# Attention probabilities of every second unit transposed by VectorE in 32x32 blocks and moved by SBUF transfers

## The chip, the cores and the metric

The kernel runs on one NeuronCore of one Trainium2 chip. The metric is the device time of one execution in microseconds (us), the median of several runs. Engines are named as the profile names them: PE is TensorE's matmuls and PEld its weight loads, DVE is VectorE, ACT is ScalarE, POOL is GpSimd, SP is SyncE, which only issues transfers.

## The reference

One encoder layer is computed for two inputs, a prompt of 1024 tokens and a sample of 512, in float32 with D_MODEL = 1024. `_token_mixer` has two branches. Branch A is grouped-query attention: 8 query heads of 64, two key/value heads, no mask. The change is in branch A.

```python
def _gqa_attention(q, k, v):
    ...
    def block(qi):
        s = jnp.einsum('bqkgd,bskd->bkgqs', qi, k, preferred_element_type=jnp.float32) * scale
        p = jax.nn.softmax(s, axis=-1)
        return jnp.einsum('bkgqs,bskd->bqkgd', p.astype(v.dtype), v)
...
    merged = jax.nn.sigmoid(ga) * (o_a @ w_proj_a) + jax.nn.sigmoid(gb) * (o_b @ w_proj_b)
    return merged @ w_out
...
    h = h + _token_mixer(_rmsnorm(h, norm_mix_g[l]), ...)
    h = h + jnp.square(jax.nn.relu(hn @ w_mlp_up[l])) @ w_mlp_down[l]
    return _rmsnorm(h, norm_final_g)
```

Branch B is attention over a neighbourhood of the token grid; a feed-forward part follows for both inputs together.

## The kernel before

Matmuls work on pairs of numbers: a value is split into a high part (a copy rounded to the type fp32r, made by ACT) and a low part (the value less the high part, a subtraction on DVE). A product takes two or three matmuls with such parts (`mm3`, lines 194 to 197, takes three).

The work runs as two trunks, first the sample (512 tokens, tile names with `s0`), then the prompt (1024 tokens, `s1`), and then the feed-forward part (`mlp`). A trunk runs branch A for its two groups of four heads (g = 0, 1), then branch B, then the merge. Each group of branch A has a stage phR, which projects and rotates queries, keys and values and writes `qT` (two tiles, one for even and one for odd heads), `kT` and `vhl`, and a stage phA, the attention, which is the stage of the change. So there are four phA stages: two for the sample, two for the prompt.

In phA a unit is one head and 512 queries: 4 units for the sample, 8 for the prompt, in the order of `units`. `NT` is the number of 128-key chunks, 4 or 8; `NB` is the number of 512-token blocks, 1 or 2.

- `s_tile(u, j)` makes the probabilities for 128 queries: score matmuls into a PSUM tile of the pool "big" (two buffers), the row maximum on DVE (line 743), the exponential on ACT (line 746, which reads PSUM and frees it), the reciprocal of the sum on DVE (line 748) and the scaling in place on POOL (line 749). The result is a P tile, 128 queries x all keys, from 8 buffers.
- For each chunk `kc` of keys, four transposes on TensorE (line 783) bring keys onto partitions, in a PSUM tile of the pool "mm" (four buffers). ACT copies the high part `hi` (`pth`, line 788, three buffers), DVE subtracts the low part `lo` (`ptl`, line 789, three buffers).
- `pv` multiplies chunk `kc` with the values, two matmuls into the unit's output (lines 759 and 760). It runs LAG = 2 chunks behind. After the last chunk `finish_o` adds both halves and stores the output.
- While a unit's chunks are worked off, `s_tile` for the next unit is put in at chunks 0, 1, 3 and 4 (prompt) or 0, 0, 1 and 2 (sample).
- `fill` gives TensorE other work between: the columns of the gate projection, generator `gate` (line 408). One `pull` is one `mm3`, three matmuls with 512 columns. A gate column has weights of its own (`w_g`, loaded on SP by `load_cols`, line 223, and cut into high and low part at lines 184 and 190) and ends each 512-token block with line 429. A phA stage works on four columns.

Large tiles come from `slot(...)`: the pool `s8r` on the right-hand side has `NRIGHT` = 11 buffers of 8 KB per partition; `slot_left` takes from another pool with 6. From the right-hand pool come `qT`, `kT`, `vhl`, the weights of the gate columns, the weights of the next stage (`wgh` and `wgl` of the second group, four tiles; `w_bq`, `w_bk` and the value strips `vs` for branch B), and for the prompt two of the eight tiles with its normalised input (`xhl`).

The order of instructions on each engine isn't the order of the program text: the framework orders the program when it is built, by priority and by its own estimate of when operands and buffers are there, and it gives a buffer to an instruction that is ready when the buffer is free, also to one that stands later in the text. Each engine then runs its list strictly in that order, and SP issues its transfers strictly in order too.

Of the kernel before, what the change touches and what calls it, by code (L numbers as in the profile page):

```python
# [15 lines left out]
ALU = mybir.AluOpType  # L16
# [45 lines left out]
def encoder(ctx: ExitStack, tc: tile.TileContext, xs, outs, w):  # L62
# [24 lines left out]
    def slot(shape, dt, name, left=False):  # L87
        return (s8l if left else s8r).tile(shape, dt, tag="s8", name=name)
# [4 lines left out]
    def mm(name):  # L93
        return pmm.tile([P, 512], F32, tag="mm", name=name)
# [301 lines left out]
    def run(tr, nxt, first):  # L396
# [100 lines left out]
        for g in range(2):  # L497
# [229 lines left out]
                setup_bias()  # L727
            with phase(f"phA{N}_{g}") as ph:
                units = [(h, qb) for h in range(4) for qb in range(NB)]
                PP = {}  # L730

                def s_tile(u, j):
                    h, qb = u
                    nm = f"{N}_{g}_{h}_{qb}_{j}"
                    q0 = (qb * 4 + j) * P
                    lhs = qT[h % 2][:, h // 2, q0 : q0 + P]
                    s = big(f"s{nm}")[:, :T]
                    for kb in range(NB):
                        ks = slice(kb * 512, kb * 512 + 512)
                        nc.tensor.matmul(s[:, ks], lhs, kT[:, 0, ks], start=True, stop=False)  # L740
                        nc.tensor.matmul(s[:, ks], lhs, kT[:, 1, ks], start=False, stop=True)  # L741
                    nm_ = sml.tile([P, 1], F32, tag="nm", name=f"nm{nm}")
                    nc.vector.tensor_reduce(nm_, s, axis=AX.X, op=ALU.max, negate=True)  # L743
                    p = ph.tile([P, T], F32, tag="P", name=f"p{nm}", bufs=8)
                    l = sml.tile([P, 1], F32, tag="l", name=f"l{nm}")
                    nc.scalar.activation(p, s, AF.Exp, bias=nm_, accum_out=l)  # L746
                    rl = sml.tile([P, 1], F32, tag="rl", name=f"rl{nm}")
                    nc.vector.reciprocal(rl, l)  # L748
                    nc.gpsimd.tensor_scalar(p, p, rl, 1.0, op0=ALU.mult, op1=ALU.mult)  # L749
                    PP[u, j] = p  # L750

                o_of = {}

                def pv(u, kc, hi, lo):
                    h, qb = u
                    if kc == 0:
                        o_of[u] = mm(f"o{N}_{g}_{h}_{qb}")
                    o = o_of[u]
                    nc.tensor.matmul(o, vhl[:, kc, :], hi, start=(kc == 0), stop=False)
                    nc.tensor.matmul(o, vhl[:, kc, :], lo, start=False, stop=(kc == NT - 1))  # L760
                    if kc == NT - 1:
                        r0 = (g * 4 + h) * HD
                        finish_o(o, 512, oad[r0 : r0 + HD, qb * 512 : qb * 512 + 512], ph, f"A{N}_{g}_{h}_{qb}")

                for j in range(4):
                    s_tile(units[0], j)
                    fill.pull(2)
                queue = []
                LAG = 2
                for ui, u in enumerate(units):  # L770
                    h, qb = u
                    if first:
                        bias_row(g * 4 + ui)
                        if g == 0 and ui == 1:
                            early["a"] = load_a(1)
                        if g == 0 and ui == 2:
                            early["v"] = load_v(1, slot)
                    nxt_u = units[ui + 1] if ui + 1 < len(units) else None
                    sdone = 0
                    for kc in range(NT):  # L780
                        pt = mm(f"pT{N}_{g}_{h}_{qb}_{kc}")
                        for j in range(4):
                            nc.tensor.transpose(  # L783
                                pt[:, j * P : (j + 1) * P], PP[u, j][:, kc * P : (kc + 1) * P], ident
                            )
                        hi = ph.tile([P, 512], F32R, tag="pth", name=f"pth{N}_{g}_{h}_{qb}_{kc}", bufs=3)
                        lo = ph.tile([P, 512], F32R, tag="ptl", name=f"ptl{N}_{g}_{h}_{qb}_{kc}", bufs=3)
                        nc.scalar.activation(hi, pt, AF.Copy)  # L788
                        nc.vector.tensor_tensor(lo, pt, hi.bitcast(F32), op=ALU.subtract)  # L789
                        queue.append((u, kc, hi, lo))  # L790
                        if nxt_u is not None:
                            while sdone < 4 and kc >= ((0, 1, 3, 4) if NB == 2 else (0, 0, 1, 2))[sdone]:
                                s_tile(nxt_u, sdone)
                                sdone += 1

                        fill.pull(1 if NB == 1 or kc % 4 < 3 else 0)
                        if len(queue) > LAG:
                            pv(*queue.pop(0))
                fill.drain()
                for item in queue:  # L800
                    pv(*item)
# [994 lines left out]
```

## Time and profile before

| | |
|---|---|
| median of 3 runs | 2145.62 us (2144.97 to 2146.48) |
| span of the profiled execution, first to last instruction | 2144.2 us |
| around that span, against the median of the runs | 1.4 us |
| mean granted TensorE clock | 0.999 |
| busy: PE, PEld, DVE, ACT, POOL | 99%, 86%, 68%, 53%, 17% |
| transposes of line 783 | 640, in 160 groups of four |
| high parts, line 788, and low parts, line 789 | 160 each |
| tiles of probabilities (line 749) | 64 of 128x1024, 32 of 128x512 |

The rows of the views are read like this. In a group's row stand the line, the engine and operation, what it writes and reads, partitions x elements and type, the count, then busy us and the mean ns of one, then the engine's idle time just before these instructions and what ended it. In a timeline's row stand the start in us from the span's start, the length, and the same names; x4 means that four instructions in a row are shown as one piece. In a row of stretches the busy us of PE, PEld, DVE, ACT and POOL follow each other with the number of instructions in brackets, then the granted clock (1.00 is full), the share of time the transfer engines were busy, and GB/s. Matmuls are pipelined, so their busy times overlap, and what a matmul costs is read from the distance of starts.

### The profile page before, as it was taken

To read this page: it belongs to the slowest core of one execution; us is meant where nothing else is said; L and a number is where in the kernel's file an instruction comes from. 1 tells how busy PE (TensorE), PEld (TensorE's weight loads), DVE (VectorE), ACT (ScalarE), POOL (GpSimd) and SP (SyncE) were. 2 spreads that over 40 slices of the span, in tenths; PEclk is the share of its full clock that TensorE was granted. 3 is DMA by queue.
4 is the path that set the end of the run, shared out by engine and by line. 5 is a ranking of instruction groups with operands and counts; after the bars stand their busy time and mean duration, and the time that the engine had idled before them with its cause. 6 is when DMAs were issued, how large, how long until landed. Compare 5 with 4: busy or idle time off the path is not lost.

```text
span 2144.2 us, 32083 instructions
## 1 busy us (share of the span) xinstructions
PE 2116.2 (99%) x10967; PEld 1847.3 (86%) x10967; DVE 1462.7 (68%) x2793; ACT 1146.2 (53%) x2511; POOL 356.1 (17%) x446
## 2 busy tenths in 40 slices
PE   9999999999999999999999999999999999999998
PEld 8888778888897888887888899999999988888886
DVE  6665786767657755656882877777777777659563
ACT  6664653767566644555530566566655643434342
POOL 2232310323232223333200200003000000000000
PEclk9999999999999999999999999999999999999999
DMA  6437557520122133444472665578545799688561
GB/s 190 133 98 212 152 162 251 186 71 25 57 79 68 42 95 108 131 118 112 140 240 103 213 194 184 171 248 205 165 142 157 256 353 343 212 279 281 165 206 59
DMA packets 321259, 354.08 MB, mean 165 GB/s; under 512 B 31551, under 2 KB 255431, under 8 KB 321095
## 3 DMA queue, kind: packets, MB, share of 16 engines
q1 hardware_dynamic: 277927, 279.65, 41.9%
q10 hardware_dynamic: 36016, 52.19, 7.0%
q0 software_dynamic: 7152, 20.19, 3.5%
q8 instruction: 87, 1.43, 0.3%
q14 instruction: 77, 0.63, 0.1%
HBM read 264.85 MB, written 87.88 MB: 165 GB/s over the span
## 4 chain that ended last, share of the span: by engine, by line
PE 67%; DVE 1%; issue 1%; DMA 0%; ACT 0%; POOL 0%; SPq 0%; POOLq 0%; ACTq 0%; DVEq 0%
PE dn L195 6%; PE dn L196 6%; PE dn L197 6%; PE ua L195 2%; PE ua L196 2%; PE ua L197 2%; PE ud L195 2%; PE ud L196 2%; PE ud L197 2%; PE uc L195 2%; PE uc L196 2%; PE uc L197 2%; PE gpss L195 2%; PE gpss L197 2%; PE gpss L196 2%; PE ops L197 1%
## 5 line engine op out<-in xcount | busy, mean ns | idle before, releaser
L197 PE MATMUL dn<-wd,al 128*128 128x512 f32 x624 | 242.8, 389 | 0.0
L196 PE MATMUL dn<-wd,ah 128*128 128x512 f32 x624 | 242.8, 389 | 0.0
L195 PE MATMUL dn<-wd,ah 128*128 128x512 f32 x624 | 242.7, 389 | 0.0
L1273 ACT ACTIVATE ah<-ar 128x512 fp32r<-128x512 f32 x168 | 104.4, 628 | 203.1 <-PE dn L196 177.1
L1274 DVE TENSOR_TENSOR al<-ar,ah 128x512 fp32r<-128x512 f32 x168 | 113.9, 685 | 71.6 <-ACT ah L1273 64.0
L197 PEld LDWEIGHTS dn<-wd,al 128*128 128x128 f32 x624 | 117.1, 188 | 24.4
L195 PEld LDWEIGHTS dn<-wd,ah 128*128 128x128 f32 x624 | 117.1, 188 | 24.3
L196 PEld LDWEIGHTS dn<-wd,ah 128*128 128x128 f32 x624 | 117.1, 188 | 24.2
L749 POOL TENSOR_SCALAR ps<-ps,rls 128x1024 f32<-128x1024 f32 (+1 forms) x96 | 96.8, 1010 | 225.7 <-DVE rls L748 200.4
L788 ACT ACTIVATE pths<-pTs 128x512 fp32r<-128x512 f32 x160 | 94.0, 597 | 74.0 <-PE pTs L783 71.9
L789 DVE TENSOR_TENSOR ptls<-pTs,pths 128x512 fp32r<-128x512 f32 x160 | 107.6, 686 | 37.7 <-ACT pths L788 36.9
L743 DVE TENSOR_REDUCE nms<-ss 128x1 f32<-128x1024 f32 (+1 forms) x96 | 99.8, 1040 | 25.6 <-PE ss L741 25.0
L195 PE MATMUL gpss<-xs_0h,w_gs 128*128 128x512 f32 x256 | 105.5, 412 | 0.5 <-DVE ot_Bs L440 0.4
L746 ACT ACTIVATE ps<-ss,nms 128x1024 f32<-128x1024 f32 (+1 forms) x96 | 93.2, 972 | 22.8 <-DVE nms L743 20.2
L783 PEld LDWEIGHTS pTs<-ident,ps 128*128 128x128 f32 x640 | 77.9, 140 | 28.5 <-POOL ps L749 4.3
L180 POOL TENSOR_TENSOR rs_f<-ms_f,mhalf 128x1 f32<-128x1 f32 x6 | 4.0, 667 | 590.7 <-DVE ms_f L176 590.7
L197 PE MATMUL gpss<-xs_0h,w_gs 128*128 128x512 f32 x256 | 101.1, 395 | 0.2 <-DVE w_gs L190 0.2
L196 PE MATMUL gpss<-xs_0l,w_gs 128*128 128x512 f32 x256 | 101.0, 394 | 0.0
L783 PE MATMUL pTs<-ident,ps 128*128 128x128 f32 x640 | 99.0, 274 | 1.3 <-DVE ptls L789 0.6
L1273 ACT ACTIVATE A<-S 128x512 fp32r<-128x512 f32 x128 | 75.9, 623 | 31.5 <-DVE S L1336 22.7
L957 POOL TENSOR_TENSOR bms<-rects,msks 128x384 f32<-128x384 f32 (+1 forms) x72 | 70.1, 977 | 129.1 <-DVE nmbs L974 107.6
L1392 ACT ACTIVATE c<-c 128x384 f32<-128x384 f32 x96 | 50.3, 524 | 69.4 <-DVE c L1391 69.3
(330 smaller groups left out, 6419.7 us busy)
## 6 DMA issues: line engine op xcount, KB each, us to landing
ar<-ud SPq DMA_DIRECT2D x120, 512.0 KB, 5.3
br<-in_w_mlp_down_dram SPq DMA_DIRECT2D x72, 512.0 KB, 5.2
rawu<-in_w_mlp_up_dram SPq DMA_DIRECT2D x64, 512.0 KB, 4.1
ud<-c ACTq DMA_DIRECT2D x128, 192.0 KB, 3.2
raw_gs<-in_w_in_dram SPq DMA_DIRECT2D x32, 512.0 KB, 4.0
zgs<-sgs ACTq DMA_DIRECT2D x48, 256.0 KB, 2.2
ud<-cs SPq DMA_DIRECT2D x64, 192.0 KB
raw_os<-in_w_out_dram SPq DMA_DIRECT2D x16, 512.0 KB, 3.9
```

What stands on the lines that cost most here:

```text
L195: nc.tensor.matmul(out, ah, bh, start=start, stop=False, **kw)
L196: nc.tensor.matmul(out, ah, bl, start=False, stop=False, **kw)
L197: nc.tensor.matmul(out, al, bh, start=False, stop=stop, **kw)
L743: nc.vector.tensor_reduce(nm_, s, axis=AX.X, op=ALU.max, negate=True)
L746: nc.scalar.activation(p, s, AF.Exp, bias=nm_, accum_out=l)
L749: nc.gpsimd.tensor_scalar(p, p, rl, 1.0, op0=ALU.mult, op1=ALU.mult)
L783: nc.tensor.transpose(pt[:, j * P : (j + 1) * P], PP[u, j][:, kc * P : (kc + 1) * P], ident)
L788: nc.scalar.activation(hi, pt, AF.Copy)
L789: nc.vector.tensor_tensor(lo, pt, hi.bitcast(F32), op=ALU.subtract)
L957: nc.gpsimd.tensor_tensor(bm.rearrange("p (r c) -> p r c", c=32), rects[h][:, ir : ir + kr_n, jr : jr + 32], msk[:, hf * 3 + ct, :].rearra ...
L1273: nc.scalar.activation(hi, src, AF.Copy)
L1274: nc.vector.tensor_tensor(lo, src, hi.bitcast(F32), op=ALU.subtract)
```

## The change

Every second unit in the order of `units` (`moved`: numbers 1, 3, 5, 7) gets its chunks of keys without TensorE and PSUM.

- The unit's four tiles of probabilities go into one tile `PM` (16 KB per partition for the prompt, one buffer), in an order in which 32-key blocks stand by their place b within a chunk, then by chunk, then by query tile j. The exponential writes in that order, the scaling on POOL is done in place as before.
- `blocks_t`: DVE transposes every 32x32 block of tile j in place (`nc.vector.transpose`).
- `spread_t`: when the fourth tile is done, transfers on SP's queue carry each of the 16 combinations of 32-partition blocks (b, a) to its partitions in a tile `PX`, 64 KB each, 2 KB per partition. There is one PX tile for four chunks, so 16 transfers for a sample unit and 32 for a prompt unit. PX tiles come from `slot`, the right-hand pool with 11 buffers.
- `chunk_hl`: for a moved unit ACT copies the high part from PX, and POOL, not DVE, subtracts the low part from PX.
- P tiles of the other units have 4 buffers, not 8.
- The order of `s_tile` becomes `ahead`: 1, 0, 3, 2, 5, 4, 7, 6. Two units are made before the first chunk (with one `pull` after each tile, eight in all as before); then a unit's probabilities are made during the chunks of the unit two earlier in that order: 3 during 0, 2 during 1, and so on.

```diff
-                PP = {}
+                PP, PX = {}, {}
+                moved = {u: i % 2 == 1 for i, u in enumerate(units)}
...
-                    p = ph.tile([P, T], F32, tag="P", name=f"p{nm}", bufs=8)
                     l = sml.tile([P, 1], F32, tag="l", name=f"l{nm}")
-                    nc.scalar.activation(p, s, AF.Exp, bias=nm_, accum_out=l)
                     rl = sml.tile([P, 1], F32, tag="rl", name=f"rl{nm}")
+                    if moved[u]:
+                        if j == 0:
+                            PP[u] = ph.tile([P, 4, NT, 4, 32], F32, tag="PM", name=f"pm{nm}", bufs=1)
+                        p = PP[u][:, :, :, j, :]
+                        nc.scalar.activation(
+                            p.rearrange("p b k i -> p k b i"),
+                            s.rearrange("p (k b i) -> p k b i", b=4, i=32),
+                            AF.Exp,
+                            bias=nm_,
+                            accum_out=l,
+                        )
+                        p = p.rearrange("p b k i -> p (b k) i")
+                    else:
+                        p = PP[u, j] = ph.tile([P, T], F32, tag="P", name=f"p{nm}", bufs=4)
+                        nc.scalar.activation(p, s, AF.Exp, bias=nm_, accum_out=l)
                     nc.vector.reciprocal(rl, l)
                     nc.gpsimd.tensor_scalar(p, p, rl, 1.0, op0=ALU.mult, op1=ALU.mult)
-                    PP[u, j] = p
+
+                def blocks_t(u, j):
+                    p = PP[u][:, :, :, j, :].rearrange("p b k i -> p (b k) i")
+                    nc.vector.transpose(p, p)
+
+                def spread_t(u):
+                    h, qb = u
+                    PX[u] = []
+                    for q in range(NT // 4):
+                        t = slot([P, 4, 4, P], F32R, f"px{N}_{g}_{h}_{qb}_{q}")
+                        PX[u].append(t.bitcast(F32))
+                        for b in range(4):
+                            for a in range(4):
+                                nc.sync.dma_start(
+                                    PX[u][q][b * 32 : b * 32 + 32, a].rearrange("p k q -> p (k q)"),
+                                    PP[u][a * 32 : a * 32 + 32, b, q * 4 : q * 4 + 4].rearrange("p k j i -> p (k j i)"),
+                                )
+
+                def chunk_hl(u, kc, hi, lo):
+                    h, qb = u
+                    if moved[u]:
+                        src = PX[u][kc // 4][:, :, kc % 4, :].rearrange("p a (j i) -> p a j i", j=4)
+                        hv, lv = (t.rearrange("p (j a i) -> p a j i", j=4, a=4) for t in (hi, lo))
+                        nc.scalar.activation(hv, src, AF.Copy)
+                        nc.gpsimd.tensor_tensor(lv, src, hv.bitcast(F32), op=ALU.subtract)
+                        return
+                    pt = mm(f"pT{N}_{g}_{h}_{qb}_{kc}")
+                    for j in range(4):
+                        nc.tensor.transpose(pt[:, j * P : (j + 1) * P], PP[u, j][:, kc * P : (kc + 1) * P], ident)
+                    nc.scalar.activation(hi, pt, AF.Copy)
+                    nc.vector.tensor_tensor(lo, pt, hi.bitcast(F32), op=ALU.subtract)
...
-                for j in range(4):
-                    s_tile(units[0], j)
-                    fill.pull(2)
+                ahead = [u for i in range(0, len(units), 2) for u in (units[i + 1], units[i])]
+
+                def s_step(u, j):
+                    s_tile(u, j)
+                    if moved[u]:
+                        blocks_t(u, j)
+                        if j == 3:
+                            spread_t(u)
+
+                for i in range(2):
+                    u = ahead.pop(0)
+                    for j in range(4):
+                        s_step(u, j)
+                        fill.pull(1)
...
-                    nxt_u = units[ui + 1] if ui + 1 < len(units) else None
+                    nxt_u = ahead.pop(0) if ahead else None
...
-                        pt = mm(f"pT{N}_{g}_{h}_{qb}_{kc}")
-                        for j in range(4):
-                            nc.tensor.transpose(
-                                pt[:, j * P : (j + 1) * P], PP[u, j][:, kc * P : (kc + 1) * P], ident
-                            )
                         hi = ph.tile([P, 512], F32R, tag="pth", name=f"pth{N}_{g}_{h}_{qb}_{kc}", bufs=3)
                         lo = ph.tile([P, 512], F32R, tag="ptl", name=f"ptl{N}_{g}_{h}_{qb}_{kc}", bufs=3)
-                        nc.scalar.activation(hi, pt, AF.Copy)
-                        nc.vector.tensor_tensor(lo, pt, hi.bitcast(F32), op=ALU.subtract)
+                        chunk_hl(u, kc, hi, lo)
...
-                                s_tile(nxt_u, sdone)
+                                s_step(nxt_u, sdone)
```

## The prediction

> **What bounds the kernel now.** I read the page first, then the busy time by stage, the instructions grouped by form in the stage of the change, TensorE's timeline, and last who held the tile buffers. The page: TensorE is busy throughout, at full clock.
>
> ```profile
> span 2144.2 us, 32083 instructions
> PE 2116.2 (99%) x10967; PEld 1847.3 (86%) x10967; DVE 1462.7 (68%) x2793; ACT 1146.2 (53%) x2511; POOL 356.1 (17%) x446
> PEclk9999999999999999999999999999999999999999
> ```
>
> Busy time in the four attention stages of branch A (two for the sample, two for the prompt; columns: stretch, length, then PE, PEld, DVE, ACT, POOL, the granted clock, the DMA share, GB/s):
>
> ```profile
> 51.90:95.40 43.50, 42.48 (x210) 32.83 (x210) 33.34 (x68) 30.47 (x64) 11.90 (x16) 1.00 0.50 149
> 130.00:171.30 41.30, 40.75 (x205) 32.30 (x206) 29.80 (x61) 27.81 (x60) 12.08 (x17) 1.00 0.43 119
> 453.70:582.40 128.70, 128.24 (x686) 104.65 (x687) 92.90 (x146) 83.41 (x147) 37.01 (x32) 1.00 0.12 37
> 645.40:774.80 129.40, 128.96 (x688) 105.03 (x688) 92.31 (x145) 84.90 (x149) 37.23 (x33) 1.00 0.17 50
> ```
>
> TensorE is the bound in all four; DVE has 72%, ACT 65%, POOL 29% of a prompt stage. What a group of four transposes costs TensorE shows in its timeline, since busy times overlap:
>
> ```profile
> 495.15 0.40 PE L760 MATMUL os<-ptls,vhls 128*128 128x512 f32 x1
> 495.39 0.60 PE L783 MATMUL pTs<-ident,ps 128*128 128x128 f32 x4
> 495.74 0.48 PE L740 MATMUL ss<-kTs,qTs 128*128 128x512 f32 x1
> 496.06 0.39 PE L741 MATMUL ss<-kTs,qTs 128*128 128x512 f32 x1
> 496.29 0.40 PE L740 MATMUL ss<-kTs,qTs 128*128 128x512 f32 x1
> ```
>
> Matmuls follow each other by 0.23 us (496.06 to 496.29). From 495.15 to 496.06 are 0.91 us; less two such steps, the four transposes take 0.45 us. A unit of the prompt has 8 groups (3.6), 16 value matmuls (3.7), 16 score matmuls (3.7) and 18 gate matmuls (4.1): 15.1 us, eight units to a stage.
>
> **What it removes.** Half of 160 groups: 80 x 0.45 = 36 us of TensorE, 14.4 in a prompt stage and 3.6 in a sample stage. A moved unit keeps 11.5 us.
>
> **What it adds and moves**, by these rows of the first prompt stage and, last, one of POOL from the feed-forward part:
>
> ```profile
> L789 DVE TENSOR_TENSOR ptls<-pTs,pths 128x512 fp32r<-128x512 f32 x64 | 42.9, 686 | 15.6 <-ACT pths L788 15.4
> L743 DVE TENSOR_REDUCE nms<-ss 128x1 f32<-128x1024 f32 x32 | 38.9, 1216 | 8.2 <-PE ss L741 8.0
> L748 DVE RECIPROCAL rls<-ls 128x1 f32<-128x1 f32 x32 | 5.1, 159 | 8.4 <-ACT ps L746 7.8
> L788 ACT ACTIVATE pths<-pTs 128x512 fp32r<-128x512 f32 x64 | 37.6, 597 | 30.2 <-PE pTs L783 29.6 <-ACT ps L746 0.2
> L746 ACT ACTIVATE ps<-ss,nms 128x1024 f32<-128x1024 f32 x32 | 35.6, 1114 | 9.4 <-DVE nms L743 7.9 <-DVE rls L748 1.3
> L746 ACT ACTIVATION_READ_ACCUMULATOR ps<-ss,nms 128x1 f32 x32 | 6.3, 196 | 0.0
> L749 POOL TENSOR_SCALAR ps<-ps,rls 128x1024 f32<-128x1024 f32 x32 | 37.0, 1156 | 84.5 <-DVE rls L748 72.1 <-DMA zgs<-sgs 11.8 <-PE pTs L783 0.6
> L184 ACT ACTIVATE wghs<-rawkvs 128x512 fp32r<-128x512 f32 x1 | 0.6, 642 | 0.0
> L342 POOL TENSOR_TENSOR B<-ta,B 128x512 fp32r<-128x512 f32 x12 | 15.5, 1295 | 120.2 <-ACT B L339 118.7 <-DMA xrs<-in_x_prompt_dram 1.2
> ```
>
> - The low parts of a moved unit go from DVE (8 x 0.686 = 5.5 us) to POOL, where the same form took 1.295: 10.4, and with four scalings of the next unit (4 x 1.156) 15.0 against TensorE's 11.5.
> - The high parts stay on ACT, now from SBUF: 0.642 for 0.597, nothing that matters.
> - The block transposes are new on DVE, four per moved unit, and no row shows one. Bounds: 0.69 (a 512-element operation) and 2.4 (twice the 1.216 of a 1024-element reduction). I take 1.2, the row of the same length. During an unmoved unit DVE then has 8 x 0.686 + 4 x (1.216 + 0.159 + 1.2) = 15.8 us against TensorE's 15.1, in a moved one little; the pair hides it.
> - The Trainium skill (VectorE: DVE Perf Modes, The three transpose paths) gives 311 ns for 128x128 in bf16; eight of them would be 2.5 us a tile, an estimate from that page, and DVE would have 21 us there instead of 15.8. No trace here shows it.
> - The exponentials write with stride into PM: between no cost and 0.2 us each; ACT has room.
> - The transfers: 16 of 64 KB for each PX tile, 32 for a moved prompt unit, all on SP's queue. Nearest are the value strips of branch B, also 64 KB over 32 partitions; the second row is their size and time from issue to landing:
>
> ```profile
> 948.71 4.60 SPq L878 DMA_DIRECT2D vss<-vds  x10
> vss<-vds SPq DMA_DIRECT2D x128, 64.0 KB, 2.3
> ```
>
> An issue takes 0.46 us. A PX tile is there after 16 x 0.46 + 2.3 = 9.7 us, both of a unit after 17.0. They wait for the transposes and for a buffer; behind them on SP stand the loads of gate weights and of the next stage.
>
> **Where the path goes.** Summed by engine, TensorE would stay the bound and the stage would lose its 14.4 us. But a moved unit is a serial chain through PM, of which there is one buffer: its four tiles are filled, transposed, carried off, and only then may the next moved unit's first exponential write. That exponential stands on ACT ahead of the high parts of the unit in work; its scores hold the two large PSUM tiles that the next unit's scores need. The chain's start shows here (first score matmul, fourth scaling):
>
> ```profile
> 453.69 0.50 PE L740 MATMUL ss<-kTs,qTs 128*128 128x512 f32 x1 [0.91 <-ACT kTs L594]
> 464.18 1.13 POOL L749 TENSOR_SCALAR ps<-ps,rls 128x1024 f32<-128x1024 f32 x1 [0.24 <-DVE rls L748]
> ```
>
> 11.6 us for four tiles from an empty start; later, with scores ready, 4 x (1.114 + 0.196) + 0.159 + 1.156 + 1.2 = 7.8, and with waits for busy POOL and DVE I take 10. With two PX tiles at hand a cycle is 10 + 17.0 = 27.0, less than the 30.2 that a pair takes now: harmless.
>
> PX tiles, however, come from the 11 right-hand buffers. In the prompt's first stage these hold two x tiles, qT (2), kT, vhl and four gate columns; the eleventh goes to the next stage's weights before the stage begins, and every one that comes free is taken so:
>
> ```profile
> 439.81 1.99 ACT L184 ACTIVATE w_gs<-raw_gs 128x1024 fp32r<-128x1024 f32 x2
> 442.93 1.09 ACT L184 ACTIVATE w_gs<-raw_gs 128x1024 fp32r<-128x1024 f32 x1
> 446.34 1.06 ACT L184 ACTIVATE wghs<-rawqs 128x1024 fp32r<-128x1024 f32 x1 [1.26 <-DMA rawqs<-in_w_in_dram]
> 506.79 0.60 ACT L429 ACTIVATE sgs<-gpss 128x512 f32<-128x512 f32 x1
> 507.29 1.05 ACT L184 ACTIVATE wghs<-rawqs 128x1024 fp32r<-128x1024 f32 x1
> 698.85 0.60 ACT L429 ACTIVATE sgs<-gpss 128x512 f32<-128x512 f32 x1
> 699.35 1.05 ACT L184 ACTIVATE w_bks<-raw_bks 128x1024 fp32r<-128x1024 f32 x1
> ```
>
> Line 429 ends a gate column's second half; 0.5 us later the next stage's weights are cut into the buffer, in both prompt stages. A PX tile is only ready to ask after its transposes; what came free before is gone. Five buffers change hands in the stage and four go to weights: one is left for PX, two once qT[0] is done (after unit 4's scores).
>
> With one buffer the second PX tile waits until the first has been used: four chunks, 0.642 + 4 x 1.295 + 2 x 0.23 = 6.3 us. A cycle is then 10 + 9.7 + 6.3 + 9.7 = 35.7.
>
> **The sum.** Prompt stage from its first scores:
> - unit 1: its second tile waits for the second gate column, behind eight score tiles (7.4 us of TensorE), 9 + 16 gate steps of 0.69 (17.3) and some chunks, 27 to 30 us; with 9.7, 40.
> - unit 3: one buffer, 35.7, and some 4 until another column ends: 40.
> - units 5 and 7: two buffers, 27 each.
> - the last four chunks and the output: 8.
>
> 142 against 128.7 and 129.4: 13 us more in each, 26. Gate matmuls fill part of the waits but are no longer there later; that is in the sum, since the chain sets it.
>
> Sample stages: one PX tile a unit, and 11 - 4 buffers. By these rows of the second one
>
> ```profile
> L749 POOL TENSOR_SCALAR ps<-ps,rls 128x512 f32<-128x512 f32 x16 | 11.3, 712 | 27.8 <-DVE rls L748 23.0 <-PE pTs L783 4.7
> L746 ACT ACTIVATE ps<-ss,nms 128x512 f32<-128x512 f32 x16 | 10.9, 687 | 2.7 <-DVE nms L743 2.7
> ```
>
> the chain is 4 x (0.687 + 0.2) + 0.16 + 0.71 + 0.7 = 5.1, with waits 7 to 8, plus 9.7; two cycles and the last chunks (8) are 43 against 43.5 and 41.3: +4 for both, with the next stage's loads late.
>
> 2144.2 + 26 + 4 = 2174; the medians' 2145.6 are 1.4 above the profiled span, and next-stage weights that are cut late may cost 2 to 3 us in all, a guess. I say 2178.
>
> **Rivals.**
> 1. One buffer throughout: weights take qT[0]'s as well. 40 + 40 + 36 + 36 + 8 = 160 a stage, +31 each: 2211. For it: the 0.5 us above. Against: by then the four weight tiles may be served. TensorE would stand idle for 5 us and more at a time. The one stretch in which it does so now is the end:
>
> ```profile
> 2136.00:2145.00 9.00, 0.00 (x0) 0.00 (x0) 2.12 (x4) 2.02 (x4) 0.55 (x1) 0.70 0.31 117
> ```
>
> No matmul, and a mean clock of 0.70 where every stage above has 1.00: after long gaps the matmuls would start slow. Between nothing and the row's 0.30 x 9 = 2.7 us a gap; at 1 to 2 us and 8 to 12 gaps 2211 becomes 2219 to 2235. The Trainium skill (TensorE: Matmul & The Clock Gate, Part 1) states the rule: an idle window of about 3.4 us halves the clock until 3.4 us are busy again. The row above agrees with the fall; by the rule a gap costs 1.7 us, an estimate from that page.
> 2. The other side, faster: PX finds two buffers each time, because weights are not cut so early once ACT, DVE and SP have other work. Then the first cycle is 13 + 17, three more 27, the rest 8: 119 a prompt stage, 10 less; sample stages +0: 2144.2 - 20 + 1.4 = 2126. It decides if the second prompt stage's cuts of `w_bks` come after unit 5. POOL's 15.0 against 11.5 in a moved unit, some 2 us of which can't overlap, gives nearly the same: 8 pairs x (3.6 - 2) + 4 x 1.8 = 20 less, 2126. Against it: the cuts above, each at once when a buffer came free.
> 3. TensorE alone decides and nothing else shows: 2144.2 - 36 + 1.4 = 2110. For it: 99%. Against: a single PM and a POOL that is fuller than TensorE in each moved unit.
> 4. Gains and waits cancel: within 0.2%, about what a measurement of this kernel can tell from no change (4 us).
>
> That the change does not do what it says is unlikely: by the code a moved unit issues no transpose on TensorE.
>
> **How the numbers follow.** The forecast (serial chain, mixed buffers) 0.57, by itself 2158 to 2204: a chain of 8 to 12 us in eight cycles is 16 us either way, a block transpose of 0.69 to 2.4 us at each chain's end 4 less or 10 more; rival 1 0.20; rival 2 0.12; rival 3 0.05; cancelling 0.04; slower in other ways (DVE at 2.4 us a transpose, late weights) 0.02. Faster 0.17, same 0.04, slower 0.79. The range from 2120 to 2232 leaves out rival 3 and the upper half of rival 1 with slow clock: under 0.2.
>
> **What would show it.** 320 transposes on TensorE in place of the 640 of line 783; four stages with less TensorE time in sum (about 305 for 340 us); 320 SP issues near 0.46 us and landings near 2.3; DVE transposes near 1.2 us; POOL's subtraction near 1.3. Right: waits of TensorE for high and low parts of moved units, long SP waits before the second PX tile, gaps of ACT before a moved unit's first exponential that a DMA ends, prompt stages of about 142 us. Wrong: prompt stages under 125 us with TensorE above 97% (rivals 2, 3); a PX tile that lands 17 us after the transposes in every unit, without a wait for a buffer (the shortage is not there); or the loss in other stages, such as the one behind, whose weights are late.

## The result, and the profile after

The changed kernel takes 2284.8 us (2283.3 to 2287.1, four runs) where the kernel before took 2145.4: 139 us more, a ratio of 1.065 (95% interval 1.0635 to 1.0665). The predicted direction was right, the size was not: 2178 was predicted, 33 us more, and 2284.8 lies far above the stated range, which ends at 2232. The page of the profile after (compare its first lines with those of before):

```profile
span 2284.4 us, 31802 instructions
PE 2160.6 (95%) x10647; PEld 1839.0 (81%) x10647; DVE 1464.7 (64%) x2761; ACT 1151.1 (50%) x2511; POOL 456.0 (20%) x526
PEclk9897999999999987999999999999999999999999
pxs<-pms SPq DMA_DIRECT2D x320, 64.0 KB, 2.0
```

320 instructions fewer on TensorE, as said, yet 44 us more of busy time: the clock row has dips where it had none. Busy time by stage, here and below from a stage's first score matmul to its last value matmul; the last line of this view sums the four stages and all their engines:

```profile
51.10:111.30 60.20, 45.87 (x173) 31.84 (x172) 30.23 (x62) 29.14 (x61) 20.89 (x24) 0.88 0.42 120
149.20:203.60 54.40, 45.98 (x173) 31.63 (x172) 27.53 (x58) 27.24 (x59) 21.81 (x25) 0.86 0.30 81
496.60:675.10 178.50, 147.12 (x613) 104.86 (x611) 96.24 (x134) 88.27 (x153) 76.71 (x64) 0.92 0.32 82
732.60:912.90 180.30, 147.24 (x561) 101.37 (x562) 95.30 (x133) 88.49 (x151) 78.02 (x65) 0.86 0.30 78
sum 473.40, PE 386.21 PEld 269.69 DVE 249.30 ACT 233.15 POOL 197.43; mean PE 96.55 PEld 67.42 DVE 62.33 ACT 58.29 POOL 49.36
```

and for the kernel before, whose stages measured in this way are 43.6, 41.4, 130.4 and 129.5 us:

```profile
sum 344.90, PE 341.51 PEld 275.39 DVE 248.63 ACT 227.47 POOL 98.22; mean PE 85.38 PEld 68.85 DVE 62.16 ACT 56.87 POOL 24.55
```

So 128.5 of the 140.2 us between the two profiled spans are lost inside the stages: 98.9 in the two of the prompt, 29.6 in the two of the sample. 11.7 lie outside them: 12.3 us were added between the sample's second stage and the prompt's first, and the other stretches nearly cancel. No engine is full any more: in a prompt stage TensorE is busy for 82%, POOL for 43%.

What the stage waits for shows on ACT. The first exponentials of the four moved units (line 751), and a gate column's end ahead of the second, from ACT's timeline; the brackets give the idle time before and what ended it:

```profile
500.59 1.12 ACT L751 ACTIVATE pms<-ss,nms 128x1024 f32<-128x1024 f32 x1 [0.54 <-DVE nms L744]
539.58 0.60 ACT L429 ACTIVATE sgs<-gpss 128x512 f32<-128x512 f32 x1 [6.43 <-PE gpss L197]
540.81 1.11 ACT L751 ACTIVATE pms<-ss,nms 128x1024 f32<-128x1024 f32 x1 [0.63 <-ACT sgs L429]
581.16 1.11 ACT L751 ACTIVATE pms<-ss,nms 128x1024 f32<-128x1024 f32 x1 [0.63 <-ACT sgs L429]
625.24 1.11 ACT L751 ACTIVATE pms<-ss,nms 128x1024 f32<-128x1024 f32 x1 [0.61 <-ACT sgs L429]
```

From one moved unit's first exponential to the next one's, called the loop from here on, pass 40.2, 40.4 and 44.1 us, and 49.9 from the last one to the stage's end at 675.10. In between the transfers run on SP:

```profile
513.22 10.02 SPq L779 DMA_DIRECT2D pxs<-pms  x16
513.22 23.14 SPq L779 DMA_DIRECT2D pxs<-pms  x32
555.18 23.90 SPq L779 DMA_DIRECT2D pxs<-pms  x32
```

Sixteen issues take 10.02 us, 0.63 each. The 32 of a unit take 23.1 (unit 1) and 23.9 (unit 3), some of it waiting. SP's three largest waits in this stage (total, times, longest):

```profile
SPq L779 <- DVE rls L762: 43.4, 2, 25.3
SPq L779 <- DVE pms L768: 34.7, 2, 18.7
SPq L779 <- DMA oads<-os_As: 10.7, 4, 3.6
```

Its long waits are for the fill (from the first exponential into PM until VectorE has transposed the fourth tile), the shorter ones for ACT's stores of outputs, which in this trace update the same completion semaphores as the transfers. No wait is for a reader of PX: no transfer waits for a buffer. So by its durations the loop is the fill, 540.81 to 555.18 = 14.4 us, the transfers 23.9, and their landing 2.0: 40.3, which fits the exponentials. But the brackets name no transfer: each of the three later exponentials comes right behind a gate column's end in ACT's list. Run 2 below shows what that means.

### The profile page after: what moved, and what is told of

Read it like the earlier page. It is cut to its first block, busy times and chain, and to the rows that moved or that the text cites. A ratio compares the mean times of both kernels' runs of the same rounds, so it can differ in the third digit from the quotient of the medians.

```text
span 2284.4 us, 31802 instructions
## 1 busy us (share of the span) xinstructions
PE 2160.6 (95%) x10647; PEld 1839.0 (81%) x10647; DVE 1464.7 (64%) x2761; ACT 1151.1 (50%) x2511; POOL 456.0 (20%) x526
## 4 chain that ended last, share of the span: by engine, by line
PE 60%; DVE 2%; POOL 2%; SPq 2%; issue 1%; ACT 1%; DMA 1%; ACTq 0%; POOLq 0%; DVEq 0%
PE dn L197 6%; PE dn L195 6%; PE dn L196 6%; PE ua L197 2%; PE ua L196 2%; PE ua L195 2%; PE ud L195 2%; PE ud L197 2%; PE ud L196 2%; PE uc L197 2%; PE uc L196 2%; PE uc L195 2%; PE gpss L195 2%; PE gpss L197 2%; PE gpss L196 2%; SPq L779 2%
## 5 line engine op out<-in xcount | busy, mean ns | idle before, releaser
L791 POOL TENSOR_TENSOR ptls<-pxs,pths 128x512 fp32r<-128x512 f32 x80 | 102.8, 1314 | 114.2 <-ACT pths L790 61.8
L741 PE MATMUL ss<-kTs,qTs 128*128 128x512 f32 x160 | 81.0, 506 | 40.8 <-ACT pms L751 21.6
L807 PE MATMUL os<-ptls,vhls 128*128 128x512 f32 x160 | 78.8, 492 | 22.7 <-POOL ptls L791 22.0
L741 PEld LDWEIGHTS ss<-kTs,qTs 128*128 128x128 f32 x160 | 36.3, 227 | 66.0 <-ACT pms L751 30.3
L1326 DVE TENSOR_TENSOR A<-S,A 128x512 fp32r<-128x512 f32 x128 | 84.5, 686 | 3.9 <-ACT A L1325 3.9
L195 PE MATMUL ud<-B,A 128*128 128x384 f32 x256 | 85.8, 335 | 0.7 <-DVE c L1443 0.7
L195 PE MATMUL uc<-B,A 128*128 128x384 f32 x256 | 85.7, 335 | 0.0
```

Of the source, the lines that this page charges most:

```text
L195: nc.tensor.matmul(out, ah, bh, start=start, stop=False, **kw)
L791: nc.gpsimd.tensor_tensor(lv, src, hv.bitcast(F32), op=ALU.subtract)
L1326: nc.vector.tensor_tensor(lo, src, hi.bitcast(F32), op=ALU.subtract)
```

## The experiments

Stages in us, before: 43.6, 41.4, 130.4, 129.5. Of run 15 only the time is used. Runs 2, 5, 6 and 9 leave out the exchange of blocks between partitions and tell of time alone. Runs 2, 4, 5, 6, 9, 10 and 13 were executed once and have no interval; the four executions of the changed kernel spread over 3.8 us.

| run | time, us | stages |
|---|---|---|
| changed kernel | 2284.8 | 60.2, 54.4, 178.5, 180.3 |
| 1 order alone | 2171.5 | 44.0, 44.0, 139.7, 140.3 |
| 2 four transfers of 256 KB a PX tile | 2282.9 | 59.0, 54.0, 179.4, 180.1 |
| 3 half of the transfers on ACT | 2248.3 | 56.6, 56.0, 168.7, 167.7 |
| 4 two PM buffers, sample only | 2281.9 | 59.8, 50.5, 178.4, 180.6 |
| 5 one transfer of 1 MB a PX tile | 2166.1 | 50.7, 48.8, 133.3, 132.4 |
| 6 as 5, low parts on VectorE | 2153.2 | 50.7, 48.4, 129.0, 128.6 |
| 7 half of the transfers on POOL | 2233.2 | 55.0, 53.6, 157.8, 165.0 |
| 8 as 7, low parts on VectorE | 2200.2 | 55.2, 47.8, 148.2, 146.8 |
| 9 as 6, order of before | 2169.2 | 51.4, 47.1, 131.2, 140.5 |
| 10 low parts on VectorE | 2244.9 | 55.7, 55.9, 167.3, 169.5 |
| 11 order of before | 2322.7 | 63.1, 62.3, 195.8, 197.0 |
| 12 as 8, order of before | 2228.3 | 55.2, 53.5, 156.0, 165.6 |
| 13 smaller buffers (control) | 2298.3 | 59.2, 59.4, 187.3, 185.0 |
| 14 as 13, two PM buffers | 2225.5 | 59.4, 49.1, 142.0, 142.3 |
| 15 as 14, half of the low parts on VectorE | 2207.8 | – |
| 16 as 14, all low parts on VectorE | 2193.8 | 56.1, 45.9, 128.7, 131.4 |
| 17 as 16, in the prompt only | 2158.8 | 45.4, 41.8, 128.6, 132.5 |

**1. The order alone.**

```diff
-                moved = {u: i % 2 == 1 for i, u in enumerate(units)}
+                moved = {u: False for u in units}
...
-                        p = PP[u, j] = ph.tile([P, T], F32, tag="P", name=f"p{nm}", bufs=4)
+                        p = PP[u, j] = ph.tile([P, T], F32, tag="P", name=f"p{nm}", bufs=8)
```

> The new order of the score tiles alone (odd unit of a pair first, two units ahead), every unit still transposed by TensorE, eight P tiles as before; nothing is moved. Theory (the serial loop of a moved unit through the one PM makes the loss): the order costs next to nothing, 2143 to 2152. Rival (the order itself makes PE wait, because scores of two units now stand ahead of a unit's value matmuls): some 10 us a prompt stage, 2160 to 2170.

2171.5, ratio 1.012 (1.0104 to 1.0138): the rival, and 1.5 us beyond its range. 23.1 us in the four stages, 9.3 and 10.8 in the prompt's. Both units of the first pair are scored before the first chunk; in the first prompt stage the first value matmul comes 24.8 us after the first score matmul (480.77 against 456.0), 16.8 in the kernel before.

**2. A quarter of the transfers.**

```diff
-                            for a in range(4):
-                                nc.sync.dma_start(PX[u][q][b * 32 : b * 32 + 32, a] ..., PP[u][a * 32 : a * 32 + 32, b, ...] ...)
+                            nc.sync.dma_start(PX[u][q][b * 32 : b * 32 + 32] ..., PP[u][b * 32 : b * 32 + 32, :, ...] ...)
```

> Same bytes moved by a quarter of the transfers: 4 of 256 KB for each PX tile in place of 16 of 64 KB. Each moves a partition block onto itself, so blocks are not exchanged between partitions, and the result is not the reference's. Theory (the loop is fill 14.4 + 32 issues x 0.633 + landing): 8 issues take 5 us if an issue has a fixed price, the loop falls from 40.3 to some 22 to 24, below TensorE's 26.6 a pair, and a prompt stage to 120 to 130 us; with the sample stages near 45 each, 2140 to 2175 in all. Rival 1 (short of right-hand buffers, as predicted): nothing changes in who holds them, 2250 or more. Rival 2 (an issue costs by its bytes): four times 0.633 each, 2280.

2282.9, and no theory had foreseen why. SP's and ACT's timelines, and size and landing of these transfers:

```profile
510.77 7.81 SPq L778 DMA_DIRECT2D pxs<-pms  x8
538.48 1.11 ACT L751 ACTIVATE pms<-ss,nms 128x1024 f32<-128x1024 f32 x1 [0.54 <-ACT sgs L429]
```

```profile
pxs<-pms SPq DMA_DIRECT2D x80, 256.0 KB, 4.8
```

The issues end at 518.6, the last lands some 4.8 us later, so PM is free by 523.4; but its next exponential comes at 538.5. ACT's list of instructions is the same in this kernel and in the changed one, entry by entry through the whole program: the builder (the framework that lays out the lists by its own estimates) seems to have taken four transfers to last as long as sixteen. In the list the exponential stands behind the first four high parts of the moved unit before it and behind two ends of gate columns, and ACT goes by the list: its gap before ends with the gate column, not with a transfer. By its durations the loop would have been shorter, and nothing was gained.

**5 and 6. Transfers that the builder, too, takes for short; and POOL's part.**

```diff
-                        for b in range(4):
-                            for a in range(4): ...
+                        nc.sync.dma_start(PX[u][q].rearrange("p a k q -> p a (k q)"), PP[u][:, :, q * 4 : q * 4 + 4] ...)
```

In 6 also `nc.gpsimd.tensor_tensor(lv, ...)` becomes `nc.vector.tensor_tensor(lv, ...)`.

> One transfer of 1 MB for each PX tile in place of 16, all 128 partitions onto themselves: the bytes are the same, the blocks are not exchanged, and the result is not the reference's. In the four-transfer run the transfers left PM 15 us before the next moved unit's exponential, which came no earlier because ACT's list, the same as in the changed kernel, has it behind the first four high parts and the gate columns. Here the list that the builder writes has that exponential ahead of the fourth high part of the unit before. Theory (the place in the lists, set by what the builder thinks the transfers take, makes the loop of 40 us): loop 27 to 30 us, prompt stages 128 to 140, 2150 to 2185 in all. Rival (something on the chip, POOL's subtractions above all, makes the loop): 40 us again, 2270 or more.

> As the run with one transfer a tile, and the low parts of moved units on VectorE in place of POOL; the blocks are not exchanged, the result is not the reference's. Theory as there; what POOL's 1.31 us a chunk costs beyond it shows as the difference: 10.5 us for eight chunks against TensorE's 11.5 leaves little, 0 to 3 us a pair, 0 to 25 us in all. Rival (POOL decides what is left): over 30 us.

2166.1 and 2153.2, both as their theories had it. With the lists changed the loop falls to 22 to 30 us. These are the first exponentials of the four moved units in run 5:

```profile
470.46 1.12 ACT L751 ACTIVATE pms<-ss,nms 128x1024 f32<-128x1024 f32 x1 [0.54 <-DVE nms L744]
492.49 1.13 ACT L751 ACTIVATE pms<-ss,nms 128x1024 f32<-128x1024 f32 x1
517.90 1.12 ACT L751 ACTIVATE pms<-ss,nms 128x1024 f32<-128x1024 f32 x1 [0.43 <-DVE nms L744]
548.03 1.11 ACT L751 ACTIVATE pms<-ss,nms 128x1024 f32<-128x1024 f32 x1 [2.74 <-DVE nms L744]
```

108 of the 128.5 us in the stages are gone. Run 5 shortens the transfers on the chip and in the lists together; run 2 shows that the first alone gains nothing. But this is still no gain over before, with 36 us of transposes removed and two issues left of a moved prompt unit's 32. Run 6 shows what stands in their place, VectorE in the middle of a prompt stage (third of the busy times):

```profile
500.00:520.00 20.00, 18.85 (x89) 14.56 (x88) 18.95 (x31) 16.10 (x29) 7.28 (x7) 1.00 0.43 145
520.00:540.00 20.00, 18.24 (x88) 13.95 (x86) 19.44 (x29) 14.81 (x25) 7.79 (x6) 1.00 0.35 125
```

19.0 and 19.4 of 20 us: here VectorE is nearly as full as TensorE was before. Over the whole first prompt stage it is busy for 112.8 of 129.0 us and TensorE for 120.7, and TensorE's direct waits for VectorE come to 3 us. So it is a reading, and not shown by a run, that VectorE now sets the stage's length.

**3, 7 and 8. All transfers, on two queues.** Every second one by `nc.scalar.dma_start` (3) or by `nc.gpsimd.dma_start` (7; 8 with the low parts on VectorE).

> Every second transfer of a PX tile is issued by ACT in place of SP. Theory (issue on one queue sets the loop): 16 issues x 0.633 = 10 us on each, loop 14.4 + 10.1 + 2 + 2 = 28 to 30, prompt stages 135 to 145 us, 2190 to 2215 in all; ACT's 10 us more a pair fit, but its own work waits behind the issues. Rival (the data movement, not the issue, sets the 0.63): both queues take 0.63 in turn or 1.2 each, 2280.

> Every second transfer issued by POOL, the others by SP; nothing left out. The list has the next moved unit's first exponentials ahead of the chunks of the unit in work. Theory: the loop falls to 14 + 10 + 4 = 28 us if POOL issues at SP's price, 35 if at 1 us each with POOL's own work behind; the gap before the prompt's first stage (293 against 282 us) goes back as SP is freer; 2180 to 2240. Rival (POOL's issues, software-made, stand in the way of its scalings and subtractions): 2270 or more.

> As the run with SP and POOL, and the low parts of moved units on VectorE, so that POOL has scalings and issues only. Theory: 5 to 20 us below that run; 2165 to 2225. Rival (POOL is not in the way): the same within 4 us.

Ratios 1.048 (1.0462 to 1.0493), 1.041 (1.0392 to 1.0423) and 1.026 (1.0240 to 1.0275). All three are faster than the changed kernel. Run 3 misses its theory's range by 33 us, 7 and 8 lie in theirs. With ACT issuing, ACT stands still for it:

```profile
525.13 8.98 ACTq L779 DMA_DIRECT2D pxs<-pms  x14
534.16 1.06 ACT L184 ACTIVATE w_gs<-raw_gs 128x1024 fp32r<-128x1024 f32 x1 [9.03 <-DMA pxs<-pms]
```

With POOL issuing it is POOL, 16 in 7.9 us, ahead of scalings and subtractions. Taking the subtractions from POOL gave 33 us more, where 5 to 20 were expected.

**10. Only the low parts back on VectorE.**

> Only the low parts of moved units go back to VectorE; 32 transfers by SP and the new order stay. Theory (the loop through PM and SP sets the stages, POOL's subtractions lie beside it except at the end of each stage and in the fill, where scalings wait for up to four subtractions of 1.25): 2 to 4 us of each fill's 14.4 and 3 to 4 at each stage's end, 15 to 30 us in all, 2255 to 2270. Rival 1 (POOL sets the stage): 2230 or less. Rival 2 (wholly beside it): within 4 us of 2284.8.

2244.9: 40 us, more than the theory's range and less than the rival's. Of the 41.3 us between the two profiled spans 25 are gained inside the stages and 16 outside them. How POOL gets into the loop shows around unit 3's fourth exponential in the changed kernel (timelines of POOL, PE and ACT):

```profile
544.49 4.98 POOL L791 TENSOR_TENSOR ptls<-pxs,pths 128x512 fp32r<-128x512 f32 x4
549.52 0.50 PE L807 MATMUL os<-ptls,vhls 128*128 128x512 f32 x1 [0.50 <-POOL ptls L791]
550.06 0.59 ACT L443 ACTIVATE ot_As<-os 64x512 f32<-64x512 f32 x1 [1.79 <-PE os L807]
550.68 1.11 ACT L751 ACTIVATE pms<-ss,nms 128x1024 f32<-128x1024 f32 x1
```

The last value matmul of the unit in work waits for POOL, ACT's copy of its output for the matmul, and the exponential stands behind the copy. Without POOL the four exponentials take 8.5 us (521.6 to 530.1) in place of 11.0. But the fill is no shorter, 14.2 (521.57 to 535.76), as VectorE now has the subtractions among its reductions and transposes. The first prompt stage's three loops gain 6 us together and its end 5. Why the weights after the sample come in time again was not isolated.

**9, 11 and 12. The order of before** (`ahead = list(units)`, one unit before the first chunk), on run 6, on the changed kernel and on run 8.

> One transfer of 1 MB a PX tile (blocks not exchanged, so the result is not the reference's), low parts on VectorE, and the order of before: one unit's scores ahead, even unit first. Theory (the new order costs some 23 us by itself, besides the transfers): 2153 falls to 2125 to 2140, below the kernel before, as 36 us of transposes are gone and little stands in their place. Rival (with tiles moved, the lead of two units is needed, or the 23 us were the eight P tiles' in that run): 2148 or more.

> The changed kernel with the order of before: even unit first, one unit ahead; everything else as changed. Theory: no lead at the start of a stage, 8 us less each in the prompt, but the transfers of a unit now lie bare between its neighbour's chunks and its own: a pair takes 15 + 3 + 22 or more, 40 to 45 us; 2270 to 2320. Rival (the order was the mistake): 2240 or less.

> Transfers by SP and POOL in turn, low parts on VectorE, order of before; nothing left out. Theory: transfers of 10 to 13 us lie bare in each pair but lead and single PM cost no more: a pair 15 + 3 + 12 + 4 = 34, prompt stages 140 to 150, 2185 to 2215, no faster than with the new order (2200). Rival (the lead was the larger part there): 2170 or less.

2169.2 (16 us slower than run 6, where 13 to 28 faster was expected), 2322.7 (ratio 1.083, 1.0812 to 1.0848) and 2228.3 (1.039, 1.0371 to 1.0402; run 8 has 1.026). The first is its rival's case, the others end 3 and 13 us above their theories' ranges. The cost of the order in run 1 does not add to the rest: with tiles that have to travel the new order, with its lead of a second unit, is 16, 38 and 28 us better than the old.

**4, 13 and 14. A second PM.** There is room for it in the sample's stages as they are (4: `bufs=2 if NB == 1 else 1`). In the prompt's it needs room: 10 right-hand buffers, two high and two low parts (`LAG = 1`), one store tile (13, PM still single; 14 with `bufs=2`).

> Two PM buffers in the two sample stages (there is room there), one in the prompt stages as before. Theory: the second moved unit's fill no longer waits for the first one's transfers; of the 60.0 and 54.2 us of the sample stages each loses 6 to 9, 2266 to 2274 in all, prompt stages unchanged near 178. Rival (something else, such as POOL's subtractions or late weights, sets the sample stages): within 3 us of 2284.8.

> Control: the changed kernel with the room for a second PM set free but not used: 10 right-hand buffers for 11, two high and two low parts for three (value matmuls one chunk behind for two), one store tile for two. Theory (PM and transfers make the loop; right-hand buffers are not short): 2280 to 2300. Rival (right-hand buffers are short, as predicted): a unit waits for its second PX tile, 8 us and more in each moved unit, 2330 or more.

> The control with a second PM buffer in all four stages; 32 transfers of 64 KB by SP and POOL's subtractions as changed. Theory (the one PM makes the loop): the fill of 14 us no longer waits for the transfers before it, the loop is SP's 32 x 0.633 + 2 = 22 to 24 or PE's 27, prompt stages 135 to 150, 2190 to 2225. Rival 1 (the transfers themselves are the bound through SP): 40 us again, 2270 or more. Rival 2 (POOL): 155 to 165 a stage, 2235 to 2260.

Against its control the second PM takes 73 us off (2298.3 to 2225.5, ratio to before 1.037, 1.0358 to 1.0389), with the same 32 transfers on SP and the same subtractions on POOL. The prompt stages, of the control first, are 45 and 43 us shorter:

```profile
497.80:685.10 187.30, 149.75 (x614) 106.67 (x612) 95.29 (x134) 89.52 (x152) 76.91 (x64) 0.92 0.30 78
742.50:927.50 185.00, 145.07 (x564) 98.61 (x565) 96.48 (x133) 89.72 (x151) 78.04 (x65) 0.90 0.29 76
493.70:635.70 142.00, 126.80 (x561) 91.67 (x559) 92.43 (x130) 87.10 (x150) 76.50 (x64) 0.97 0.36 94
702.80:845.10 142.30, 127.42 (x568) 93.06 (x569) 91.17 (x129) 86.14 (x149) 77.12 (x65) 0.99 0.35 93
```

So in the prompt the loop does run through the one PM; a second one changes the durations and the lists together, and no run tells the two apart here. The sample's first stage stays as it was (59.2 and 59.4; 60.2 and 59.8 in run 4), the second loses 10.3 us against the control and 3.9 in run 4, whose time of 2281.9 is its rival's case. All in all the stages of run 14 lose 98 us against the control's, but the span only 72: 26 us come back outside them, in part where TensorE waits for the next stage's weights, behind the sample's second stage and behind the prompt's second:

```profile
PE pqbs L195 <- ACT w_bqs L184: 13.5, 1, 13.5
PE pkbs L195 <- ACT w_bks L184: 7.5, 1, 7.5
```

In the control the first of these waits takes 4.2 us and the second is not there. And the control shows that right-hand buffers are not short: with 10 instead of 11 the prompt stages took 9 and 5 us more, the other smaller buffers included.

**15, 16 and 17. What is left.** Every second low part on VectorE, then all of them, then moved units in the prompt only.

> The run with two PM buffers, and every second low part of a moved unit on VectorE, the others on POOL. Theory: POOL has 5.2 of 10.5 us less a moved unit and its scalings come earlier, VectorE has 2.8 more; 5 to 20 us below that run, 2175 to 2215. Rival (POOL is not in the way once PM is double): within 4 us of it.

> The run with two PM buffers, and all low parts on VectorE. Theory: VectorE then has 113 us of work in a prompt stage, as in the run with one transfer a tile and low parts on it (129 us a stage): prompt stages 132 to 142, 2165 to 2200. Rival (SP's transfers bound it): as the run with two PM buffers within 4 us. A gain over the kernel before would need prompt stages under 129, which the runs so far do not promise.

> The best complete variant so far (two PM buffers, low parts on VectorE, smaller buffers elsewhere) with moved units in the prompt only; the sample's stages have the order, the P tiles and the transposes of before. Theory (VectorE takes over as the bound of a prompt stage: 109 of 129 us there, so nothing is left of the 14.4 us that TensorE saves): sample stages 44 to 47 us, prompt stages 127 to 133, late weights some us, 2148 to 2165. Rival (the gain shows once the sample's losses are out): 2140 or less.

2207.8 (ratio 1.029, 1.0271 to 1.0305), 2193.8 (1.023, 1.0209 to 1.0244) and 2158.8 (1.006, 1.0044 to 1.0078). The last one's prompt stages:

```profile
451.90:580.50 128.60, 122.64 (x561) 92.98 (x558) 109.34 (x161) 86.91 (x150) 39.73 (x32) 0.97 0.39 100
648.10:780.60 132.50, 126.91 (x573) 96.76 (x574) 109.60 (x161) 86.52 (x150) 40.34 (x33) 0.96 0.39 99
```

Together 261.1 us, 259.9 before: with PM doubled and POOL relieved the moved units cost nothing in the prompt, and bring nothing. VectorE has 109 us there for 93. The rest lies around them: 2 us in the sample's stages, 4.7 more between the prompt's, and 6.8 behind the second, where TensorE waits for the next weights. All three lie in their theories' ranges, and no variant beat the kernel before.

## Why the prediction was right or wrong

- **The engines' prices by rows held.** First prompt stage of the changed kernel, by form:

```profile
L791 POOL TENSOR_TENSOR ptls<-pxs,pths 128x512 fp32r<-128x512 f32 x32 | 41.1, 1314 | 44.5 <-ACT pths L790 27.7 <-DMA pxs<-pms 16.8
L768 DVE STREAM_TRANSPOSE pms<-pms 128x1024 f32<-128x1024 f32 x16 | 19.6, 1236 | 3.0 <-POOL pms L763 2.0 <-DMA zgs<-sgs 0.2
L790 ACT ACTIVATE pths<-pxs 128x512 fp32r<-128x512 f32 x32 | 18.7, 625 | 10.1 <-PE os L806 5.5 <-POOL ptls L791 2.9 <-DVE ptls L797 0.9
L751 ACT ACTIVATE pms<-ss,nms 128x1024 f32<-128x1024 f32 x16 | 17.8, 1113 | 7.0 <-DVE nms L744 5.0 <-ACT sgs L429 1.9
```

  POOL 1.314 (1.295 predicted), block transpose 1.236 (1.2), high part 0.625 (0.642), strided exponential 1.113, the 1.114 of before. The estimate of 2.5 from the Trainium skill (VectorE: DVE Perf Modes, The three transpose paths) was twice the measured one.
- **The step that failed: "with two PX tiles at hand a cycle is 10 + 17.0 = 27.0 ... harmless".** With two PX tiles at hand it was 40.3. The fill took 14.4, not 10, and 12.6 even at the start of the stage (500.59 to 513.22): its tiles take turns on ACT and VectorE with the neighbouring units', and taking POOL out of it (run 10) left 14.2. The 32 transfers took 23.9 + 2.0, not 17.0: an issue took 0.63, not the 0.46 of the value strips' row (5 us over 32 issues), and some 3 us went into waits on ACT's stores, which the prediction had not thought of. Of the 13.3 us between 27.0 and 40.3 the fill has 4.4, the transfers 8.9.
- **Two cycles were right for a wrong reason.** 40 was predicted for units 1 and 3, from a missing PX buffer, and 40.2 and 40.4 measured; but no transfer waited for a buffer. So units 5 and 7, forecast at 27 each with 8 for the end (62), took 44.1 and 49.9 (94). That and 4 us ahead of the first exponential are the prompt stages' 178.5 in place of 142. That run 14, with a double PM, has stages of 142 us is chance: there the first exponentials lie 18, 28 and 34 us apart, not 40, 40 and 27.
- **Rival 2 had the right condition and the wrong time.** It was to be decided by whether the next stage's weights are cut late, `w_bks` in the second prompt stage after unit 5. They are: in the first prompt stage ACT cuts `wghs` at 652.89 where it was 446.34 and 507.29, in the second `w_bks` at 904.01, after unit 5 and even after unit 7, whose first exponential stands at 862.67:

```profile
652.89 1.05 ACT L184 ACTIVATE wghs<-rawqs 128x1024 fp32r<-128x1024 f32 x1
904.01 1.04 ACT L184 ACTIVATE w_bks<-raw_bks 128x1024 fp32r<-128x1024 f32 x1
```

  PX found its buffers each time, as the rival said. Its 2126 did not follow, because it too reckoned a cycle at 27. Of the forecast's signs, the long waits of SP before the second PX tile did not show, and only one gap of ACT ahead of a moved unit's first exponential ends with a transfer (0.6 us, in the second prompt stage).
- **What the sum of durations could not see: the place in the lists.** In the changed kernel the loop by durations and the place in ACT's list agree within 3 us (unit 1's last issue ends at 536.4, landing 2.0; exponential at 540.81), so either would give 40. Run 2 shows that the lists alone are enough to hold it there.
- **Sample stages: +4 predicted, +29.6 measured.** Three are the order (run 1); with short transfers 14.5 are left (run 5); a second PM changes 4. Which waits make up the rest was not isolated.
- **Late weights: a guess of 2 to 3 us, 11.7 measured outside the stages.** The largest wait of TensorE between the sample's second stage and the prompt's first:

```profile
PE pqbs L195 <- ACT w_bqs L184: 5.9, 1, 5.9
```

  The load of these weights stood on SP behind the last transfers of the second sample stage and the value strips: the queue was counted in the prediction, what it holds up was not.
- **TensorE's signs.** 320 transposes, as said; but 386 us of busy time in the four stages where 305 was forecast, in part because matmuls ran slow: by the clock column some 109 of the stages' 473 us were at half clock, an estimate. Rival 1 had the slow clock (0.86 to 0.92 in these stages) and put 8 to 24 us on it; no run separates its cost. Its other half, one PX buffer throughout, and rival 3 did not happen.
- **A reading that was off.** The prompt's first stage before begins with a score matmul at 452.07 us, not at 453.69: it takes 130.4 us, and four tiles from an empty start 13.2. That moves the forecast by under 2 us.

## What to carry to other kernels

When a step moves off a busy engine into a chain through one buffer, add up the whole loop (fill, every issue on its queue, landing, and what each in-order engine does in between) and compare it with the time in which it has to hide; a second buffer was worth 73 us here, and shorter transfers that left the lists as they were nothing. In a program whose lists are laid out ahead of time, look where the waiting instruction stands in its engine's list: a resource that comes free early helps only if the list uses it. And see what the relieved engine's neighbour gets: of the 36 us taken from TensorE nothing showed as a gain even in the best variants, while VectorE went from 93 to 109 us and more of a prompt stage; that the one is the cause of the other was not tested.

## What the runs showed of the hardware

**A short gap was enough for the slow clock.** The granted clock changes in steps of 3.41 us. Five such windows in the first prompt stage of the changed kernel (length, then PE's busy time first, the clock before the last two numbers):

```profile
536.62:540.03 3.41, 2.92 (x13) 2.07 (x12) 0.00 (x0) 0.45 (x1) 0.00 (x0) 1.00 0.09 22
540.03:543.45 3.42, 1.38 (x5) 0.97 (x6) 0.33 (x2) 2.79 (x6) 1.14 (x2) 1.00 0.20 77
543.45:546.86 3.41, 3.03 (x7) 1.50 (x6) 3.32 (x3) 1.85 (x4) 3.41 (x3) 0.50 0.01 2
546.86:550.27 3.41, 2.38 (x8) 1.25 (x8) 1.46 (x3) 1.42 (x3) 3.41 (x4) 1.00 0.00 0
```

In the second window TensorE was idle for 2.0 of 3.4 us (40% busy), and the third ran at half clock. In the changed kernel, up to the end of branch A's last attention stage, the next window ran at half clock after all 12 full-clock windows that were less than 45% busy, after 11 of 21 with 45 to 65%, and after none above that. The Trainium skill (TensorE: Matmul & The Clock Gate, Part 1) has the fall after an idle window of about 3.4 us; the trace agrees with the length of the window, not with its having to be idle.

**An issue's price is hardly one of bytes.** On SP 64 KB between SBUF partitions took 0.63 us to issue, 256 KB 0.98 (7.81 for 8, run 2), 1 MB over all 128 partitions 0.65 (1.31 for 2, run 5). POOL issued 64 KB faster than SP, 0.49 each (run 7):

```profile
520.12 7.90 POOL L779 DMA_DIRECT2D pxs<-pms  x16 [0.31 <-DVE pms L768]
```
